# Residual loads and stores of two image pairs at a time in a DMA-bound 3x3 convolution with residual add

## Chip, cores, metric

The kernel runs on one core of a Trainium2 chip. Its time is device time in microseconds (us), the median of several executions. The span is the part of it that the profile covers, from the first to the last instruction recorded. "Outside the span" below is the measured time less the span of the same execution. The runs list every execution's span to 0.1 us; the trace of the profiled execution has it to the nanosecond. The granted clock is the share of its full clock that the tensor engine was allowed, as the trace records it. HBM is the memory off the core, SBUF the core's own (128 partitions in these tiles), and PSUM takes the tensor engine's results here. An execution counts as slow here when it is over 1.5% above the fastest of its kernel.

## The reference

A 3x3 convolution with padding 1 on 16 images of 64 channels and 64x64 pixels, float32, plus a residual of the output's shape.

```python
x_pad = np.pad(x, ((0, 0), (0, 0), (1, 1), (1, 1)))
for b, co, ci, kh, kw in ...:        # 16, 64, 64, 3, 3
    output[b, co] += weight[co, ci, kh, kw] * x_pad[b, ci, kh:kh+h, kw:kw+w]
return output + residual
```

x, residual and output are 16.8 MB each. Every byte crosses between HBM and SBUF once, so 50.3 MB plus 0.15 MB of weights have to move, whatever the order (the profile before has 50.48 MB in its packets).

## The kernel before

The images go through in 8 pairs: 128 partitions hold 2 images of 64 channels, with 4096 pixels (16 KB) in a row. ScalarE casts x to bf16, the tensor engine convolves an image into PSUM, VectorE adds the residual in its own buffer (`ro`), and that buffer is stored. The kernel holds all 8 residual buffers in SBUF at once (16.8 MB). The SP queue issues 25 of the 26 transfers.

```python
ro = [pool.tile([128, NPIX], FP32, name=f"ro{p}") for p in range(NPAIR)]     # 8 pairs
xr = [nc.alloc_sbuf_tensor(f"xr{i}", [128, NPIX], FP32) for i in range(NXR)] # 3 x buffers
...
s_r = [sem(f"s_r{p}") for p in range(NPAIR)]      # one semaphore for each residual
...
for p in range(NPAIR):
    if p >= NXR:
        nc.sync.wait_ge(s_half, 2 * (p - NXR) + 3)   # the x buffer is free again
    ...                                              # x of pair 0 and the weights go first
    load_x(p)                                        # 2 MB
    load_ro(p)                                       # 2 MB
for p in range(NEARLY):                              # 6 early stores
    nc.sync.wait_ge(s_add, 2 * p + 3)
    store(p).then_inc(s_out, 16)
...
for n in range(B):                                   # VectorE, image by image
    if im == 0:
        nc.vector.wait_ge(s_r[p], 16)
    for par in range(2):
        i = nc.vector.tensor_tensor(out=o4[...], in0=psj[...], in1=o4[...], op=ADD)
...
for p in range(NEARLY, NPAIR):                       # the last two pairs
    store(p)
with tc.tile_critical(sync_engine=mybir.EngineType.Pool, no_gpsimd_drain=True):
    nc.gpsimd.wait_ge(s_out, 16 * NEARLY)            # (cuts are marked with ...)
```

Of the kernel before, what the change touches and what calls it, by code (L numbers as in the profile page):

```python
# [8 lines left out]
FP32 = mybir.dt.float32  # L9
# [6 lines left out]
def kernel(  # L16
# [7 lines left out]
    nc = tc.nc  # L24

    B, C, H, W = x.shape
# [4 lines left out]
    NPIX = H * W  # L31
    NPAIR = B // 2
# [2 lines left out]
    NCHUNK = J // JC  # L35
    NXR = 3
    NXP = 4
    NEARLY = 6

    res_bc = residual.rearrange("b c h w -> (b c) (h w)")  # L40
    out_bc = out.rearrange("b c h w -> (b c) (h w)")
    x_bc = x.rearrange("b c h w -> (b c) (h w)")
    w_rows = weight.rearrange("co (h ci) kh kw -> (co h) (ci kh kw)", h=2)

    pool = ctx.enter_context(tc.tile_pool(name="pool", bufs=1))
    psum = ctx.enter_context(tc.tile_pool(name="psum", bufs=1, space=bass.MemoryType.PSUM))

    ident = pool.tile([128, 128], FP32)
    ro = [pool.tile([128, NPIX], FP32, name=f"ro{p}") for p in range(NPAIR)]
    xr = [nc.alloc_sbuf_tensor(f"xr{i}", [128, NPIX], FP32) for i in range(NXR)]  # L50

    xp = [pool.tile([128, J + 1, W], BF16, name=f"xp{i}") for i in range(NXP)]
# [4 lines left out]
    sem = lambda name: tc.alloc_semaphore(name)  # L57
    s_w = sem("s_w")
    s_x = [sem(f"s_x{i}") for i in range(NXR)]
    s_r = [sem(f"s_r{p}") for p in range(NPAIR)]  # L60
    s_out = sem("s_out")
    s_id = sem("s_id")
    s_wt = sem("s_wt")
    s_half = sem("s_half")
    s_pack = sem("s_pack")
    s_bank = sem("s_bank")
# [1 line left out]
    s_add = sem("s_add")  # L68

    def load_x(p, engine=nc.sync, cols=slice(0, NPIX)):  # L70
        return engine.dma_start(out=xr[p % NXR][:, cols], in_=x_bc[128 * p : 128 * p + 128, cols]).then_inc(
            s_x[p % NXR], 16
        )

    def load_ro(p):
        nc.sync.dma_start(out=ro[p][:, :], in_=res_bc[128 * p : 128 * p + 128, :]).then_inc(s_r[p], 16)

    def store(p):
        return nc.sync.dma_start(out=out_bc[128 * p : 128 * p + 128, :], in_=ro[p][:, :])

    def matmul(out_, lhsT, rhs, start, stop, ldweights):

# [18 lines left out]
    def to_the_front(dma):  # L101



        def fixed(ap):
            t = ap.bass_ap.tensor.name
            return mybir.PhysicalAccessPattern(
                ap=ap.ap, offset=ap.bass_ap.offset, dtype=ap.dtype, memref=t, memsetref=t + "_set", bass_ap=ap.bass_ap
            )

        front = nc.main_func.blocks[0].instructions
        here = nc.cur_bb.bb.instructions
        ins = here.pop()
        assert ins.name == dma.ins.name
        at = next(
            i for i, e in enumerate(front) if e.engine == ins.engine and isinstance(e, mybir.InstDrain)
        )
        front.insert(at, copy.replace(ins, ins=[fixed(a) for a in ins.ins], outs=[fixed(a) for a in ins.outs]))
# [5 lines left out]
    def weight_block(h, half, d, par, kh):  # L124

        at = 64 * half + 32 * h
        return dict(out=wl[at : at + 32, d, :, par, :], in_=tp[0:32, kh, 0:384].rearrange("p (kw co h) -> p kw co h", kw=3, h=2)[:, :, :, h])

    with tc.tile_critical(no_gpsimd_drain=True):  # L129

        for p in range(NPAIR):
            if p >= NXR:

                nc.sync.wait_ge(s_half, 2 * (p - NXR) + 3)
            if p == 0:
                to_the_front(load_x(p, cols=slice(0, NPIX // 2)))
                nc.sync.dma_start(out=wraw[:, :], in_=w_rows[:, :]).then_inc(s_w, 16)
            else:
                load_x(p)
            load_ro(p)  # L140
        for p in range(NEARLY):
            nc.sync.wait_ge(s_add, 2 * p + 3)
            store(p).then_inc(s_out, 16)


        nc.gpsimd.memset(ident[:, :], 0.0).then_inc(s_id, 1)  # L146
        nc.gpsimd.wait_ge(s_id, 1)
        nc.gpsimd.affine_select(  # L148
            out=ident[:, :],
            in_=ident[:, :],  # L150
            compare_op=mybir.AluOpType.not_equal,
            fill=1.0,
            base=0,
            pattern=[[-1, 128]],
            channel_multiplier=1,
        ).then_inc(s_id, 1)
        nc.gpsimd.wait_ge(s_id, 2)
        for t in xp:
            nc.gpsimd.memset(t[0:64, 0, :], 0.0).then_inc(s_id, 1)  # L159
            nc.gpsimd.memset(t[64:128, J, :], 0.0).then_inc(s_id, 1)  # L160
        nc.gpsimd.memset(wl[0:64, 0, :, 1, :], 0.0).then_inc(s_id, 1)  # L161
        nc.gpsimd.memset(wl[64:128, 1, :, 0, :], 0.0).then_inc(s_id, 1)  # L162


        to_the_front(load_x(0, nc.scalar, slice(NPIX // 2, NPIX)))
        for n in range(B):
            p, im = divmod(n, 2)
            hp = slice(64 * im, 64 * im + 64)
            x4 = xr[p % NXR].rearrange("q (j two w) -> q j two w", two=2, w=W)
            t = xp[n % NXP]  # L170
            if im == 0:
                nc.scalar.wait_ge(s_x[p % NXR], 16 * (p // NXR + 1 + (p % NXR == 0)))
            i = nc.scalar.copy(out=t[64:128, 0:J, :], in_=x4[hp, :, 0, :])  # L173
            i.then_inc(s_half, 1)
            if n >= NXP:
                i._wait_ge(s_conv, n - NXP + 1)
            nc.scalar.copy(out=t[0:64, 1 : J + 1, :], in_=x4[hp, :, 1, :]).then_inc(s_pack, 1)  # L177
            if n == 0:
                nc.scalar.wait_ge(s_wt, 1)
                for b in blocks[4:]:  # L180
                    for h in range(2):
                        i = nc.scalar.copy(**weight_block(h, *b))  # L182
                i.then_inc(s_wt, 1)


        nc.vector.wait_ge(s_wt, 1)
        for k, b in enumerate(blocks[:4]):
            for h in range(2):
                i = nc.vector.tensor_copy(**weight_block(h, *b))  # L189
                if k == h == 0:  # L190
                    i.then_inc(s_bank, 2)
        i.then_inc(s_wt, 1)
        for n in range(B):
            p, im = divmod(n, 2)
            hp = slice(64 * im, 64 * im + 64)
            o4 = ro[p].rearrange("q (j two w) -> q j two w", two=2, w=W)
            psj = ps[n % 2].rearrange("q c j w -> q (c j) w")
            if im == 0:
                nc.vector.wait_ge(s_r[p], 16)
            for par in range(2):  # L200
                i = nc.vector.tensor_tensor(  # L201
                    out=o4[hp, :, par, :], in0=psj[64 * par : 64 * par + 64, :, :], in1=o4[hp, :, par, :], op=ADD
                )
                if par == 0:
                    i._wait_ge(s_conv, n + 1)

                i.then_inc(s_add if par == 0 or n == B - 1 else s_bank, 1)


        nc.tensor.wait_ge(s_id, 4 + 2 * NXP)  # L210
        nc.tensor.wait_ge(s_w, 16)
        wraw3 = wraw.rearrange("p (ci t) -> p ci t", t=9)
        for t in range(9):
            i = nc.tensor.transpose(  # L214
                out=tp[0:32, t // 3, 128 * (t % 3) : 128 * (t % 3) + 128], in_=wraw3[:, :, t], identity=ident[:, :]
            )
        i.then_inc(s_wt, 1)
        nc.tensor.wait_ge(s_wt, 3)
        with nc.Fori(0, B // NXP, 1, engines=[PE]):
            for n in range(NXP):  # L220
                nc.tensor.wait_ge(s_bank, 1).then_inc(s_bank, -1)
                nc.tensor.wait_ge(s_pack, 1).then_inc(s_pack, -1)  # L222
                order = [(1, 0), (1, 1), (0, 0), (0, 1), (2, 0), (2, 1)]
                for i, (kw, d) in enumerate(order):
                    xlo, xhi = max(0, 1 - kw), min(W, W + 1 - kw)
                    for c in range(NCHUNK):
                        j0 = JC * c
                        m = matmul(
                            ps[n % 2][:, c, :, xlo:xhi],
                            wl[:, d, kw, :, :].rearrange("q r c -> q (r c)"),  # L230
                            xp[n][:, j0 + d : j0 + d + JC, xlo + kw - 1 : xhi + kw - 1],
                            i == 0,
                            i == len(order) - 1,
                            c == 0,
                        )
                m.then_inc(s_conv, 1)


    for p in range(NEARLY, NPAIR):
        store(p)  # L240
    with tc.tile_critical(sync_engine=mybir.EngineType.Pool, no_gpsimd_drain=True):
        nc.gpsimd.wait_ge(s_out, 16 * NEARLY)

# [29 lines left out]
```

## Time and profile before

| | before |
|---|---|
| time, median (first 3 executions) | 122.96 us |
| span of the profiled execution | 121.2 us |
| outside the span (same execution) | 123.0 - 121.2 = 1.8 us |
| bytes moved | 50.48 MB |
| rate, 4 to 76 us and 82 to 119 us | 432 and 431 GB/s |
| tensor engine busy, ends at | 72%, about 100 us |
| VectorE's last add ends at | 104.1 us |
| arrival of the last store: mean of the 16 DMA engines, slowest | 119.87, 120.21 us |

To read it: compute is over at 104 us, and the remaining 16 us are stores that wait in a full queue (the last two are issued at 104.4 and 104.8 us). The time goes by bytes divided by a rate that hardly varies in the two long stretches (432 and 431 GB/s). The last row comes from the trace's records of semaphore increments by the DMA engines: each of the 26 transfers ends in 16 of them (416 small packets in all), taken here as one from each of the 16 engines, and it counts as landed with the slowest.

### The profile page before, as it was taken

The numbers are of one execution on the slowest core, as the hardware profiler recorded it, in microseconds if no ns is written. First come the engines' busy times: TensorE is split into PE (matmuls) and PEld (weight loads), VectorE is DVE, ScalarE is ACT, GpSimd is POOL, SyncE is SP. The second block draws the span as 40 slices with busy tenths as digits, with TensorE's granted clock in tenths as the row PEclk, the third lists the DMA queues.
The fourth block names the chain that finished last, engine by engine and source line by source line (L and its number), as shares of the span: only waits on it lengthen the run. The fifth ranks groups of instructions, "written<-read, shape, count | busy, mean of one in ns | idle before, by whom it ended". The sixth has DMA issues, their size and how long they took to land.

```text
span 121.2 us, 736 instructions
## 1 busy us (share of the span) xinstructions
PE 87.7 (72%) x389; PEld 10.7 (9%) x105; DVE 76.0 (63%) x40; ACT 63.1 (52%) x37; POOL 2.4 (2%) x16
## 2 busy tenths in 40 slices
PE   0033499999999999999999999999999980000000
PEld 0021001101010101010101010101010100000000
DVE  0005300889898898989889898898989889300000
ACT  4049969938966984993993994896000000000000
POOL 5200000000000000000000000000000000000000
PEclk9999999999999999999999999999999999755555
DMA  6999999999999999999999999999999999999993
GB/s 168 427 444 433 433 433 433 433 427 433 433 427 427 433 433 427 427 433 427 433 433 433 433 433 422 433 389 433 433 433 433 422 433 433 433 433 433 427 433 151
DMA packets 3744, 50.48 MB, mean 417 GB/s; under 512 B 416, under 2 KB 544, under 8 KB 544
## 3 DMA queue, kind: packets, MB, share of 16 engines
q1 hardware_dynamic: 3600, 49.43, 96.3%
q10 hardware_dynamic: 144, 1.05, 2.0%
HBM read 33.70 MB, written 16.78 MB: 417 GB/s over the span
## 4 chain that ended last, share of the span: by engine, by line
PE 71%; DVEq 2%; DVE 2%; issue 0%
PE ps L86 53%; PE ps L85 17%; DVEq L129 2%; DVE ro L201 2%
## 5 line engine op out<-in xcount | busy, mean ns | idle before, releaser
L201 DVE TENSOR_TENSOR ro<-ps,ro 64x2048 f32<-64x2048 f32 x32 | 73.2, 2289 | 17.7 <-PE ps L86 17.2
L86 PE MATMUL ps<-xp,wl 128*128 128x504 bf16 (+1 forms) x288 | 80.0, 388 | 0.2
L173 ACT CAST xp<-xr 64x2048 bf16<-64x2048 f32 x16 | 30.3, 1896 | 19.3 <-DMA xr<-in_x_dram 17.1
L85 PE MATMUL ps<-xp,wl 128*128 128x504 bf16 (+1 forms) x92 | 35.8, 389 | 3.4 <-PEq L222 3.4
L177 ACT CAST xp<-xr 64x2048 bf16<-64x2048 f32 x16 | 30.4, 1897 | 0.4
L85 PEld LDWEIGHTS ps<-xp,wl 128*128 128x128 bf16 x96 | 9.5, 99 | 79.1 <-issue 79.1
L189 DVE CAST wl<-ps 32x192 bf16<-32x192 f32 x8 | 2.8, 348 | 10.4 <-PE ps L214 10.3
L214 PE MATMUL ps<-ident,wraw 128*32 128x128 f32 x9 | 2.1, 412 | 8.1 <-DMA wraw<-in_weight_dram 8.1
L214 PEld LDWEIGHTS ps<-ident,wraw 128*32 128x32 f32 x9 | 1.2, 137 | 8.6 <-issue 8.1
L173 ACT ACT_TABLE_LOAD x1 | 1.3, 1283 | 1.1 <-SPq L129 1.1
L182 ACT CAST wl<-ps 32x192 bf16<-32x192 f32 x4 | 1.2, 306 | 0.0
L160 POOL MEMSET xp<- 64x64 bf16 x4 | 0.6, 147 | 0.2
L159 POOL MEMSET xp<- 64x64 bf16 x4 | 0.6, 145 | 0.2
L148 POOL TENSOR_SCALAR_AFFINE_SELECT ident<-ident 128x128 f32<-128x128 f32 x1 | 0.3, 295 | 0.2 <-POOL ident L146 0.2
L162 POOL MEMSET wl<- 64x192 bf16 x1 | 0.3, 253 | 0.1
L161 POOL MEMSET wl<- 64x192 bf16 x1 | 0.3, 252 | 0.1
L146 POOL MEMSET ident<- 128x128 f32 x1 | 0.2, 205 | 0.7 <-SPq L129 0.7
L257 POOL MEMSET const-uint8-127<- 128x1 uint8 x1 | 0.1, 113 | 0.0
L257 POOL MEMSET const-bfloat16-1.0<- 128x1 bf16 x1 | 0.1, 112 | 0.0
L257 POOL MEMSET const-float32-1.0<- 128x1 f32 x1 | 0.1, 109 | 0.0
L257 POOL MEMSET const-float32-0.0<- 128x1 f32 x1 | 0.1, 104 | 0.2 <-issue 0.2
## 6 DMA issues: line engine op xcount, KB each, us to landing
ro<-in_residual_dram SPq DMA_DIRECT2D x8, 2048.0 KB, 21.9
out_dram<-ro SPq DMA_DIRECT2D x8, 2048.0 KB, 28.2
xr<-in_x_dram SPq DMA_DIRECT2D x7, 2048.0 KB, 17.5
xr<-in_x_dram SPq DMA_DIRECT2D x1, 1024.0 KB, 7.0
xr<-in_x_dram ACTq DMA_DIRECT2D x1, 1024.0 KB, 7.6
wraw<-in_weight_dram SPq DMA_DIRECT2D x1, 144.0 KB, 6.9
```

The lines of the kernel that those rows point to most:

```text
L85: return e.matmul(out=out_, lhsT=lhsT, rhs=rhs, start=start, stop=stop, skip_group_check=True)
L86: return e.add_instruction(mybir.InstMatmult(name=nc.get_next_instruction_name(), engine=PE, ins=[e.lower_ap(rhs), e.lower_ap(lhsT)], outs ...
L129: with tc.tile_critical(no_gpsimd_drain=True):
L159: nc.gpsimd.memset(t[0:64, 0, :], 0.0).then_inc(s_id, 1)
L160: nc.gpsimd.memset(t[64:128, J, :], 0.0).then_inc(s_id, 1)
L173: i = nc.scalar.copy(out=t[64:128, 0:J, :], in_=x4[hp, :, 0, :])
L177: nc.scalar.copy(out=t[0:64, 1 : J + 1, :], in_=x4[hp, :, 1, :]).then_inc(s_pack, 1)
L182: i = nc.scalar.copy(**weight_block(h, *b))
L189: i = nc.vector.tensor_copy(**weight_block(h, *b))
L201: i = nc.vector.tensor_tensor(out=o4[hp, :, par, :], in0=psj[64 * par : 64 * par + 64, :, :], in1=o4[hp, :, par, :], op=ADD)
L214: i = nc.tensor.transpose(out=tp[0:32, t // 3, 128 * (t % 3) : 128 * (t % 3) + 128], in_=wraw3[:, :, t], identity=ident[:, :])
L257: nc = _bacc.Bacc("TRN2", target_bir_lowering=False, num_devices=1)
```

## The change

The intent: fewer, larger transfers (residuals of pairs 2-3, 4-5 and 6-7 in one load of 4 MB each; pairs 0-1, 2-3 and 4-5 in one store of 4 MB each), x of the odd pairs loaded one transfer earlier, the last two pairs still stored one by one, and fewer semaphores to clear. Cut to its core:

```diff
-    NEARLY = 6
-    res_bc = residual.rearrange("b c h w -> (b c) (h w)")
+    NEARLY = 3
+    RES = (slice(0, 1), slice(1, 2), slice(2, 4), slice(4, 6), slice(6, 8))
+    res_bc = residual.rearrange("(p b) c h w -> (b c) p (h w)", b=2)
-    ro = [pool.tile([128, NPIX], FP32, name=f"ro{p}") for p in range(NPAIR)]
+    ro = pool.tile([128, NPAIR, NPIX], FP32)
-    s_r = [sem(f"s_r{p}") for p in range(NPAIR)]
+    s_r = [sem(f"s_r{i}") for i in range(2)]
-    s_wt = sem("s_wt")                  # its counts move to s_id
...
+    def load_ro(i):
+        if i >= 2:
+            nc.sync.wait_ge(s_r[i % 2], 16 * (i // 2))
+        nc.sync.dma_start(out=ro[:, RES[i], :], in_=res_bc[:, RES[i], :]).then_inc(s_r[i % 2], 16)
+    def store(pairs):
+        return nc.sync.dma_start(out=out_bc[:, pairs, :], in_=ro[:, pairs, :])
...
-            load_ro(p)
-        for p in range(NEARLY):
-            nc.sync.wait_ge(s_add, 2 * p + 3)
-            store(p).then_inc(s_out, 16)
+            if p in (0, 1, 3, 5, 7):
+                load_ro((p + 1) // 2)
+        for k in range(NEARLY):
+            nc.sync.wait_ge(s_add, 4 * k + 5)
+            store(slice(2 * k, 2 * k + 2)).then_inc(s_out, 16)
...
-    for p in range(NEARLY, NPAIR):
-        store(p)
+    for p in range(2 * NEARLY, NPAIR):
+        store(slice(p, p + 1))
```

More of the change, by code (lines that the diff above doesn't have):

```diff
@@ L37 @@
     NXP = 4
-    NEARLY = 6
-    res_bc = residual.rearrange("b c h w -> (b c) (h w)")
-    out_bc = out.rearrange("b c h w -> (b c) (h w)")
+    NZERO = 4 + 2 * NXP
+    NEARLY = 3
+    RES = (slice(0, 1), slice(1, 2), slice(2, 4), slice(4, 6), slice(6, 8))
+    res_bc = residual.rearrange("(p b) c h w -> (b c) p (h w)", b=2)
+    out_bc = out.rearrange("(p b) c h w -> (b c) p (h w)", b=2)
     x_bc = x.rearrange("b c h w -> (b c) (h w)")
@@ L73, in load_x @@
         )
-    def load_ro(p):
-        nc.sync.dma_start(out=ro[p][:, :], in_=res_bc[128 * p : 128 * p + 128, :]).then_inc(s_r[p], 16)
-    def store(p):
-        return nc.sync.dma_start(out=out_bc[128 * p : 128 * p + 128, :], in_=ro[p][:, :])
+    def load_ro(i):
[4 more added lines that the diff above has]
+        return nc.sync.dma_start(out=out_bc[:, pairs, :], in_=ro[:, pairs, :])
     def matmul(out_, lhsT, rhs, start, stop, ldweights):
@@ L178 @@
             if n == 0:
-                nc.scalar.wait_ge(s_wt, 1)
+                nc.scalar.wait_ge(s_id, NZERO + 1)
                 for b in blocks[4:]:
@@ L182 @@
                         i = nc.scalar.copy(**weight_block(h, *b))
-                i.then_inc(s_wt, 1)
-        nc.vector.wait_ge(s_wt, 1)
+                i.then_inc(s_id, 1)
+        nc.vector.wait_ge(s_id, NZERO + 1)
         for k, b in enumerate(blocks[:4]):
@@ L191 @@
                     i.then_inc(s_bank, 2)
-        i.then_inc(s_wt, 1)
+        i.then_inc(s_id, 1)
+        first = [pairs.start for pairs in RES]
         for n in range(B):
@@ L195 @@
             hp = slice(64 * im, 64 * im + 64)
-            o4 = ro[p].rearrange("q (j two w) -> q j two w", two=2, w=W)
+            o4 = ro[:, p, :].rearrange("q (j two w) -> q j two w", two=2, w=W)
             psj = ps[n % 2].rearrange("q c j w -> q (c j) w")
-            if im == 0:
-                nc.vector.wait_ge(s_r[p], 16)
+            if im == 0 and p in first:
+                i = first.index(p)
+                nc.vector.wait_ge(s_r[i % 2], 16 * (i // 2 + 1))
             for par in range(2):
@@ L207 @@
                 i.then_inc(s_add if par == 0 or n == B - 1 else s_bank, 1)
-        nc.tensor.wait_ge(s_id, 4 + 2 * NXP)
+        nc.tensor.wait_ge(s_id, NZERO)
         nc.tensor.wait_ge(s_w, 16)
@@ L216 @@
             )
-        i.then_inc(s_wt, 1)
-        nc.tensor.wait_ge(s_wt, 3)
+        i.then_inc(s_id, 1)
+        nc.tensor.wait_ge(s_id, NZERO + 3)
         with nc.Fori(0, B // NXP, 1, engines=[PE]):
```

## The prediction

> **What bounds the kernel now.** I read the summary by engine and by slice first. The tensor engine is busy for 72% of the span and nothing else on chip reaches that, but the row to read is the one of the DMA engines:
>
> ```profile
> PE   0033499999999999999999999999999980000000
> ...
> DMA  6999999999999999999999999999999999999993
> GB/s 168 427 444 433 433 433 433 433 427 433 433 427 427 433 433 427 427 433 427 433 433 433 433 433 422 433 389 433 433 433 433 422 433 433 433 433 433 427 433 151
> ```
>
> The tensor engine ends in slice 33 of 40, at about 100 us; the DMA engines run at the same rate from the second slice to the last but one. So the bytes are the clock of this kernel. Next come the DMA queues, and then the busy time by stretch:
>
> ```profile
> DMA packets 3744, 50.48 MB, mean 417 GB/s; under 512 B 416, under 2 KB 544, under 8 KB 544
> ...
> q1 hardware_dynamic: 3600, 49.43, 96.3%
> q10 hardware_dynamic: 144, 1.05, 2.0%
> ```
>
> ```profile
> core 0: us, PE busy (x) PEld busy (x) DVE busy (x) ACT busy (x) POOL busy (x), PEclk, DMA share, GB/s
> 0.00:4.00 4.00, 0.00 (x0) 0.00 (x0) 0.00 (x0) 1.28 (x1) 2.32 (x16) 1.00 0.73 231
> 4.00:76.00 72.00, 64.26 (x283) 8.14 (x79) 50.94 (x30) 54.24 (x32) 0.07 (x1) 1.00 1.01 432
> 76.00:82.00 6.00, 6.00 (x29) 0.68 (x7) 5.39 (x3) 5.69 (x3) 0.00 (x0) 1.00 0.98 396
> 82.00:119.00 37.00, 17.43 (x80) 1.85 (x19) 19.69 (x9) 1.90 (x2) 0.00 (x0) 0.80 1.01 431
> 119.00:121.20 2.20, 0.00 (x0) 0.00 (x0) 0.00 (x0) 0.00 (x0) 0.00 (x0) 0.50 0.09 37
> ```
>
> The last two columns say that the 16 engines are fully busy (share 1.01) at 431 to 432 GB/s from 4 to 76 us and from 82 to 119 us. There are three losses: the first microseconds (231 GB/s), the change from loads to stores between 76 and 82 us (396 GB/s), and about 2 us at the end. The chain that ended last is of little use here. It names tensor lines for 71%, and then at 104 us it meets the vector engine and stops, because the final stores are behind it:
>
> ```profile
> PE ps L86 53%; PE ps L85 17%; DVEq L129 2%; DVE ro L201 2%
> ```
>
> The waits of the queue that issues the DMAs complete the picture: it waits for buffers and results, while its earlier transfers keep the engines fed.
>
> ```profile
> SPq L71 <- ACT xp L173: 51.4, 5, 15.7
> SPq L79 <- DVE ro L201: 24.9, 4, 10.0
> ```
>
> The trace's landing records give each transfer's arrival. Residual pair 2 lands at 32.33 us, x of pair 3 at 37.23, residual pair 3 at 42.08, x of pair 4 at 46.98, residual pair 7 at 81.26, and the eight stores at 86.18, 91.04, 95.91, 100.77, 105.63, 110.50, 115.36 and 120.21. In steady state a 2 MB transfer lands every 4.86 us: 2.097 MB / 4.864 us = 431 GB/s, the rate of the stretch table. There is one exception, the last load (81.26 - 76.18 = 5.08 us).
>
> [...] 8 residual loads, 8 stores, 9 x loads and 1 weight load are 26 transfers, and 26 x 16 = 416 packets, exactly the count under 512 B. [...] with the queue full, 2 MB transfers land 4.86 us apart, which is 8 packets of 16 KB per engine at 608 to 611 ns. [...]
>
> **The change part by part.**
>
> *Fewer, larger transfers.* Residual loads go from 8 to 5 and stores from 8 to 5 (three of 4 MB, two of 2 MB), so 26 transfers become 20. The data is the same, in the same 16 KB rows (each partition's row of one image channel), so 3,200 of 3,200 data packets should stay. What goes is 6 x 16 = 96 semaphore packets. In the trace's packet records one takes 9 ns, so each of the 16 engines saves 6 x 9 = 54 ns. The bubble around it cannot be much more, as 8 x 608 ns = 4.864 us is already the whole landing interval. I count **0.05 us**. The queue's issue instructions (332 to 580 ns each) become fewer and perhaps longer, but they are hidden behind full queues: the final stores, issued at 104.4 and 104.8 us, wait for their predecessors, which land until 110.5.
>
> *x loads further ahead.* The order was x0 r0 x1 r1 x2 r2 x3 r3 x4 r4 ...; it becomes x0 r0 x1 r1 x2 x3 r23 x4 x5 r45 x6 x7 r67. So x of pairs 3, 5 and 7 arrives one transfer (4.86 us) earlier, the even ones at the same time. Residual pairs come only with the second of the two. r23 lands at 42.08 us (as residual 3 did) and the vector engine first needs it for image 4: its adds start every 5.19 us from 21.72 us, so at 42.46 us. It arrives 0.38 us early, the tightest spot of the plan. r45 lands at about 61.5 for image 8 at 63.21, r67 at about 81.2 for image 12 at 83.96. So the tensor engine's pace should not change, and an earlier x only lengthens ScalarE's idle time elsewhere: it waits 17.1 us for x now, and the tensor engine does not wait for it after the start.
>
> *Stores of two pairs.* A store of 4 MB may start when its second pair is added. All loads stand ahead in the queue until 81.2 us. By then the first two are ready (after images 4 and 8, about 45 and 66 us), and they carry 4 x 4.86 = 19.5 us of transfer, to about 100.6. The third needs image 12's first half, which is added at 83.96 + 2.28 = 86.2 us: 14 us early. It reaches to about 110.3; the single last stores are issued near 104.5, so there is 5.8 us of reserve and no hole. Storing the last pairs singly keeps this: both are issued as before.
>
> *13 semaphores instead of 20.* Waiting on a merged semaphore costs the same instruction. The two transfers that wait for an earlier residual (r23 for r0, and so on) wait for things landed long before. At the end Pool clears the range of semaphores in one instruction, on the path to the span's end:
>
> ```profile
> L268 POOLq EVENT_SEMAPHORE_RANGE_CLEAR  x1: 200/200/200, 120.7 to 120.7; - x1
> ```
>
> If its 200 ns scales with the number (the records name semaphores from 96 to 127, some 30), 7 fewer are 7/30 x 200 = 47 ns; if it is fixed, nothing. I count half, **0.03 us**.
>
> *Unchanged:* the start (x0, weights, residual 0 and 1 in the same order), the turn from loads to stores (packet records: the packets that start from 76 to 80 us take 0.38 us per engine more than at 608 ns, once), the 0.34 us from the last packet's end at 119.87 to its landing at 120.21, the closing barriers, and the 1.8 us between the span of 121.2 and the measured 123.0 us.
>
> Sum: 122.96 - 0.05 - 0.03 = 122.88; I lean a little lower for small things at the turn, **122.85 us**.
>
> **The rivals.**
> *A fixed cost per transfer really is in series.* Then six fewer transfers would save six times it[...]. The landing intervals and a DMA share of 1.01 speak against it, as there is no idle time to win.
> *The larger transfers leave a hole.* If r23 came late, or a 4 MB store waited too long, the queue would run dry. A late r23 first delays the vector engine, which has 0.57 us to spare per image, then the tensor engine; only a delay of over 5 us would reach the last stores. A slip of a few tenths is likely, a hole is not; a badly timed one would make perhaps 124 to 126 us.
> *Two rows 2 MB apart in one transfer run slower in HBM.* A partition now has two 16 KB rows 2 MB apart. If packets took 1% longer, 33.5 MB or 78 us of transfer would add up to 0.8 us, 123.7. Against: the engines run at one rate for reads and writes alike (432 and 431 GB/s), so the memory's side does not seem to bind.
> *The turn from loads to stores gets cheaper or dearer.* Its whole loss is 0.4 us, so 122.5 to 123.2.
>
> **Range and chances.** The three runs before lie within 0.18 us. The expected gain of 0.1 us is below what matters, and only the second and third rival move more than the noise. I take 122.5 to 123.2 us, with 1% for faster by over 2% (under 120.5, which needs bytes to vanish or a much better rate) and 1% for slower by over 2% (over 125.4, which needs a hole of 2.4 us).
>
> **What would show it.** In the profile of the changed kernel: under 512 B 320 packets instead of 416; 50.48 MB as before; DMA share 1.01 and 431 to 432 GB/s from 4 to 76 and from 82 to 119 us; the vector engine's adds still 5.19 us apart with image 4 at 42.5 us; last add over at 104.1; the range clear at 200 ns or about 150; span 121.0 to 121.2. I am wrong if the landing interval of 2 MB shrinks below 4.8 us, if the DMA row shows a slice under 9 between 81 and 118 us, or if the vector engine waits for the residual at image 4.

Cuts in it are marked: passages on how the hardware behaves that no trace or run of this case shows, among them a size for the cost per transfer of the first rival. The sum: 122.96 - 0.05 - 0.03 = 122.88, leaned to 122.85 us, with the 0.05 from packets of 9 ns and the 0.03 from the 200 ns of the clear, both of the trace before. That a wait on a merged semaphore costs nothing more, merged_13 below (ratio 1.0007) bears out.

## The result, and the profile after

The changed kernel took 123.17 us in the median of 6 runs (122.97 to 123.42), the kernel before 123.00 us beside it (6 runs, 122.86 to 123.52). The ratio is 1.0008, with a 95% interval of 0.9985 to 1.0031: the same. A ratio is the mean time of one kernel's fast runs over that of the other's of the same rounds, so it is not quite the ratio of the medians. The repetition on another chip with more runs gave 1.0019 (1.0005 to 1.0032). The time lies in the predicted range, but near its upper end, and the small gain that was forecast is not there.

The summary by slice, of the changed kernel (tenths of each slice busy, then GB/s):

```profile
PE   0023499999999997999999999999999960000000
...
DMA  6999999999999999999999999999999999999992
GB/s 184 416 443 427 432 432 427 432 432 432 432 432 432 432 432 432 432 432 432 432 427 432 432 432 432 432 389 432 432 432 432 432 432 432 432 432 427 432 432 108
```

Its DMA queues (packets, bytes, share of the engines' span), and its stretches (the columns are those of the prediction's table; the last two are DMA share and GB/s):

```profile
DMA packets 3648, 50.48 MB, mean 416 GB/s; under 512 B 320, under 2 KB 448, under 8 KB 448
...
q1 hardware_dynamic: 3504, 49.43, 96.1%
q10 hardware_dynamic: 144, 1.05, 2.1%
```

```profile
0.00:4.00 4.00, 0.00 (x0) 0.00 (x0) 0.00 (x0) 1.28 (x1) 2.33 (x16) 1.00 0.75 238
4.00:76.00 72.00, 63.74 (x287) 8.10 (x79) 51.31 (x30) 56.02 (x33) 0.06 (x1) 1.00 1.01 432
76.00:82.00 6.00, 6.00 (x29) 0.68 (x7) 5.39 (x3) 5.58 (x4) 0.00 (x0) 1.00 1.00 410
82.00:119.00 37.00, 17.12 (x80) 1.85 (x19) 19.33 (x9) 0.23 (x1) 0.00 (x0) 0.77 1.01 431
119.00:121.20 2.20, 0.00 (x0) 0.00 (x0) 0.00 (x0) 0.00 (x0) 0.00 (x0) 0.50 0.02 7
```

The picture is the same as before. There are 96 small packets fewer, the rate of the two long stretches is the same to 1 GB/s, and there is no hole anywhere. The turn from loads to stores (76 to 82 us) moves 410 instead of 396 GB/s, and after 119 us there is less left to do (7 instead of 37 GB/s, which over 2.2 us is 0.07 MB less), so the engines are ahead on average. The chain that ended last is again cut at the final stores (and reaches back only to 47 us, 43% on tensor lines instead of 71%); the lines below show it, then the waits of the issuing queue, and the clear of the semaphores:

```profile
PE ps L89 32%; PE ps L88 11%; DVEq L132 2%; DVE ro L207 2%
```

```profile
SPq L72 <- ACT xp L177: 50.6, 5, 16.0
SPq L82 <- DVE ro L207: 27.5, 2, 20.3
```

```profile
L274 POOLq EVENT_SEMAPHORE_RANGE_CLEAR  x1: 158/158/158, 120.8 to 120.8; - x1
```

The clear takes 158 instead of 200 ns. One line is new, in the waits of the engines (total, times, longest):

```profile
DVE ro L207 <- PE ps L89: 15.3, 14, 7.3
...
DVE ro L207 <- DMA ro<-in_residual_dram: 1.4, 1, 1.4
```

VectorE waited 1.4 us for a residual, once, at image 4. That residual (pairs 2 and 3) landed at 42.09 us as predicted (42.08), but in this execution the tensor engine was ahead: the first add began at 20.57 us instead of 21.72. The matmuls of 17 to 20 us (third column: time and number), before and then after, show why:

```profile
17.00:20.00 3.00, 3.00 (x11) 0.24 (x2) 0.00 (x0) 2.19 (x2) 0.00 (x0) 1.00 1.02 437
```

```profile
17.00:20.00 3.00, 3.00 (x16) 0.29 (x3) 0.00 (x0) 2.16 (x2) 0.00 (x0) 1.00 0.99 426
```

In the same 3 us 16 matmuls begin instead of 11: the full rate came earlier. (The column with the granted clock prints 1.00 in both rows because it has no record yet; the trace's first record of a full clock is at 19.10 us before and at 16.73 after.) The earlier clock is not the change: the same program with seven unused semaphores (pad_7 below) has its full clock from 19.40 us and 10 matmuls there, its adds start at 21.85 us, and it does not wait at image 4. The wait needs both, an early clock and the late residual of the change: order_only below, which loads residual 2 alone, starts its adds at 20.75 us and waits for no residual. Over the profiles the first record of a full clock lies between 16.69 and 19.40 us. The wait moved the later adds by 0.8 us (20.57 + 15 x 5.187 = 98.37 us would be the start of the last image, 99.16 was measured), and it cost nothing at the end: the last add still ended at 103.77 us, earlier than before (104.13).

**Where the time went.** Nothing of the above explains why the measured time is 0.17 us more. The listed spans show where it is. On the chip of the repetition:

| | measured, mean | span, mean | outside the span |
|---|---|---|---|
| before (11 runs) | 123.13 | 121.32 | 1.81 (1.78 to 1.87) |
| changed (6 runs) | 123.31 | 121.22 | 2.10 (2.02 to 2.15) |

Within the span the change gains 0.10 us, close to the 0.08 predicted, but with a standard error of 0.08 us (from the listed spans), so by itself this gain is not clear of noise. Outside the span it loses 0.29 us, in every execution, and no range overlaps. The listed spans are rounded; with the exact spans of the fourteen profiled executions (experiments included) the time outside is 1.79 to 1.83 us in the six that load one residual pair at a time and 2.06 to 2.07 in the eight that load two or three, a loss of about 0.24. So the loss is 0.24 to 0.29 us. The experiments look for what does that, and test the bound itself.

### The profile page after: what moved, and what is told of

It reads as the page before. It is cut to its first block, busy times and chain, and to the rows that moved or that the text cites. A ratio compares the mean times of both kernels' runs of the same rounds, so it can differ in the third digit from the quotient of the medians.

```text
span 121.3 us, 731 instructions
## 1 busy us (share of the span) xinstructions
PE 86.9 (72%) x393; PEld 10.6 (9%) x105; DVE 76.0 (63%) x40; ACT 63.1 (52%) x37; POOL 2.4 (2%) x16
```

## The experiments

The theory: bytes at a fixed rate set the span; the number of transfers and their order hardly matter. Its main rival: a fixed cost for each transfer, in series. When the loss outside the span appeared, two further theories stood against each other: the semaphores do it, or the transfers of two pairs do.

### split_halves: 64-partition transfers (an experiment that tested something else)

```diff
-        nc.sync.dma_start(out=ro[p][:, :], in_=res_bc[128 * p : 128 * p + 128, :]).then_inc(s_r[p], 16)
+        for h in (0, 64):
+            nc.sync.dma_start(
+                out=ro[p][h : h + 64, :], in_=res_bc[128 * p + h : 128 * p + h + 64, :]
+            ).then_inc(s_r[p], 16)
```

(from the kernel before; not shown: stores likewise, counts of the waits doubled)

> Edit of the kernel before: every residual load and every store is cut into two transfers of 64 partitions (1 MB each), so 42 transfers instead of 26, with the same 16 KB rows. Theory (the bytes set the time, a transfer costs each engine only its 9 ns semaphore packet): 16 x 9 = 0.14 us more, 123.1 us, 672 small packets instead of 416, a DMA share still at 1.01. Rival (a cost per transfer that stands in series): 16 times that cost; at 0.5 us it would be 131 us[...].

Measured: 171.58 us in the median, ratio 1.378 (1.370 to 1.386) from fast runs. Two of its six runs are fast (168.46 and 170.82), the profiled one is slow (172.11). At first sight this is the rival's victory, but the stretches of its profile say otherwise:

```profile
8.00:12.00 4.00, 2.08 (x9) 1.16 (x9) 0.92 (x3) 3.82 (x3) 0.00 (x0) 1.00 1.01 213
12.00:16.00 4.00, 1.64 (x4) 0.26 (x2) 1.86 (x6) 3.92 (x6) 0.00 (x0) 1.00 1.08 225
...
156.00:160.00 4.00, 0.00 (x0) 0.00 (x0) 0.00 (x0) 0.00 (x0) 0.00 (x0) 0.50 1.02 434
```

While residual halves are loaded (first two rows) the engines are busy all the time (share 1.01 and 1.08; a packet's time is counted where it starts, so a share can pass 1) at half the rate, 213 to 225 GB/s. A cost in series for each transfer should, by the author's reasoning, have left the engines idle. The packet records agree: while residual halves move, a 16 KB packet takes some 1250 ns instead of 611. Why a load of 64 partitions goes at half the rate is not shown. The stores in halves (last row) ran at 422 to 438 GB/s from 148 us on, with packets of 611 ns, while the 16 engines were up to 5.9 us apart (one landing runs from 156.15 to 162.05 us); so the halving is shown for the loads, and why late stores escape it is not shown either. So the split changed more than the count, and the question went to col_split.

### col_split: the same count, all 128 partitions

```diff
-        nc.sync.dma_start(out=ro[p][:, :], in_=res_bc[128 * p : 128 * p + 128, :]).then_inc(s_r[p], 16)
+        for c in (slice(0, NPIX // 2), slice(NPIX // 2, NPIX)):
+            nc.sync.dma_start(out=ro[p][:, c], in_=res_bc[128 * p : 128 * p + 128, c]).then_inc(s_r[p], 16)
```

(from the kernel before; not shown: stores likewise, counts of the waits doubled)

> Edit of the kernel before: every residual load and store is cut in two by columns, over all 128 partitions (1 MB, rows of 8 KB), so again 42 transfers instead of 26. It repeats split_halves without its fault: there 64-partition transfers took 1250 ns for a 16 KB packet in place of 611. Theory (a transfer costs 9 ns per engine): 0.14 us for 16 more transfers, and 256 packets of 8 KB per engine at 309 ns in place of 128 of 16 KB at 611 ns, 0.9 us: 123.2 + 1.0 = 124.2 us at most. Rival (0.5 us or more per transfer in series): 131 us or more.

Measured: 123.44 us, ratio 1.0023 (1.0004 to 1.0041), span 121.60 instead of 121.34 us on average. Its packets:

```profile
DMA packets 6048, 50.48 MB, mean 415 GB/s; under 512 B 672, under 2 KB 800, under 8 KB 800
```

Sixteen transfers more, and twice as many data packets of half the size, cost 0.26 us together, 16 ns a transfer if all of it is laid on the count. The rival of a serial cost of half a microsecond or more is out. This is why six transfers fewer can bring so little.

### order_only: the new order of loads alone

```diff
-            load_ro(p)
+            if p < 2:
+                load_ro(p)
+            elif p % 2:
+                load_ro(p - 1)
+                load_ro(p)
```

> Edit of the kernel before: the order of loads of the changed kernel (x further ahead, residuals two by two) but as single 2 MB transfers with their own semaphores; stores as before. Theory: 123.0 us, the time does not depend on the order. Residual 2 lands at about 37.2 us instead of 42.1 in the changed kernel, so the vector engine does not wait for a residual at image 4, unlike in the changed kernel (1.4 us there). Rival (the order of loads cost what the fewer packets saved): 123.1 us or more, with the spread of the engines of the changed kernel.

Measured: 123.16 us, ratio 1.0007 (0.9991 to 1.0023), outside the span 1.80 us. Residual 2 landed at 37.33 us and VectorE waited for no residual. "x loads further ahead" is worth nothing measurable here (the rival's "123.1 us or more" is no sign of it: the kernel before took 123.18 beside it). The loss outside the span does not come from the order.

### after_again: the changed kernel once more

> The changed kernel once more, unedited, for a tighter ratio and a second profile. Theory: 0.999 to 1.001. In the first profiles the 16 engines finished their last data packet at 119.52 us on average before and 119.34 after, but the slowest one at 119.87 before and 120.00 after. If that spread comes from how a single execution starts, this profile has another spread (first to last arrival of the x of pair 0 between 0.5 and 0.9 us) and the average stays at 119.3 to 119.4. If the change makes the spread, it is again 0.8 us after the start and 0.98 us for the stores.

Measured: 123.33 us, ratio 1.0019 (1.0005 to 1.0032). Its ratio is a little above the expected bound of 1.001. The 16 engines finished the first x within 0.60 us of each other this time (0.73 in the first profile), and the last store within 0.78 us (0.98); the mean over the engines of the last data packet's end was 119.25 us, the slowest 119.81. So the spread of the first profile belonged at least in part to that execution.

### res_three: how much delay the compute side can take

```diff
-    RES = (slice(0, 1), slice(1, 2), slice(2, 4), slice(4, 6), slice(6, 8))
+    RES = (slice(0, 1), slice(1, 2), slice(2, 5), slice(5, 6), slice(6, 8))
```

> Edit of the changed kernel: residual pairs 2, 3 and 4 in one transfer of 6 MB. Theory (compute has about 5.8 us of reserve before the last two stores would find the queue empty): the transfer lands at about 46.95 us, the vector engine waits for it some 5 us at image 4, the last add ends at about 108.7 us instead of 103.8, store of pair 6 is issued at about 109.0 and its data can start about 1 us later, just when the queue empties (110.0): 122.9 to 123.4 us. Rival (a wait of the vector engine for a residual goes straight to the end): 5 us more, 128 us.

Measured: 125.50 us, ratio 1.017 (1.0138 to 1.0201), so more than the theory's 123.4 and less than the rival's 128. The load landed at 46.96 us as expected, but the last add ended at 111.02 us, not at 108.7. The stretches (third column tensor engine, then from the right GB/s, DMA share, granted clock):

```profile
48.00:52.00 4.00, 0.00 (x0) 0.07 (x1) 3.94 (x3) 0.08 (x1) 0.00 (x0) 0.75 0.99 422
52.00:56.00 4.00, 3.67 (x9) 0.33 (x3) 3.97 (x2) 3.95 (x3) 0.00 (x0) 0.50 1.04 446
...
108.00:112.00 4.00, 0.00 (x0) 0.00 (x0) 2.99 (x2) 0.00 (x0) 0.00 (x0) 0.93 0.33 139
```

The tensor engine was idle for 4.6 us, and restarted at half its clock (0.50): 9 matmuls began in 4 us. The clock records have it at half from 50.00 to 56.82 us. The half clock cost about 2.9 us on top of the wait: the adds of images 5 and 6 are 8.04 us apart, not 5.19. The store of pair 6 was issued at 111.31 us, and between 108 and 112 us the queue ran dry (share 0.33). The span of this execution is 123.41 us; that of after_again, on the same chip, is 121.22 on average, 2.19 us less. So the store could have been issued until about 111.31 - 2.19 = 109.12 us without loss. Against pad_7 below, an undelayed kernel whose adds start at the same time (21.85 us) and which issues this store at 104.56, that is an estimated reserve of 4.6 us; the prediction had 5.8 us, and left out that data follow an issue by about 1 us (the first packet of the span starts 1.01 us after the first issue, that of this store 0.85 us after its issue). The mechanism holds in these two kernels: the late residual cost nothing at the end in the changed one (a wait of 1.4 us, last add at 103.77 us), while here, together with the half clock after it, it cost 2.19 us of the span, as the final stores found the queue empty.

### pad_7, merged_13, sems_40: do the semaphores make the loss outside the span?

pad_7, from the changed kernel (back to 20 semaphores):

```diff
+    unused = [sem(f"unused{i}") for i in range(7)]
```

> What is to be explained: in eleven timed executions of the kernel before on one chip the measured time less the span is 1.78 to 1.87 us, in six of the changed kernel 2.02 to 2.15 us, so the changed kernel gains some 0.2 us within the span and gives back 0.3 us outside it; the kernel with only the new order of loads has 1.78 to 1.84. Edit of the changed kernel: 7 unused semaphores are added, so 20 again. Theory A (the number or numbering of semaphores sets the time outside the span): back to 1.8 us outside, range clear back to 200 ns, total 122.85 to 122.95 us. Theory B (the 4 MB transfers or the program's layout set it): stays at 2.1 us, total 123.3 us.

merged_13, from the kernel before (down to 13):

```diff
-    s_r = [sem(f"s_r{p}") for p in range(NPAIR)]
+    s_r = [sem(f"s_r{i}") for i in range(2)]
-    s_wt = sem("s_wt")                  # its counts move to s_id, as in the change
...
+        if p >= 2:
+            nc.sync.wait_ge(s_r[p % 2], 16 * (p // 2))
...
```

(not shown: the counts that the other engines wait for)

> Edit of the kernel before: its 20 semaphores are merged into 13 exactly as in the changed kernel (two for the residuals, the one of the weights joined to the one of the zeros), transfers and their order unchanged. Theory A (semaphores set the time outside the span): 2.1 us outside, range clear 158 ns, total 123.35 us. Theory B (4 MB transfers or layout): 1.8 us outside, total 123.1 us.

sems_40, from the changed kernel, the line of pad_7 with 40:

> Edit of the changed kernel: 40 unused semaphores are added. If the range clear goes by number, at (200 - 158) / 7 = 6 ns each, it takes 158 + 240 = 398 ns, all of it in the span; if it is a step or fixed it stays near 158 to 200 ns. Time outside the span: with theory A it differs from 2.1 us, with theory B it is 2.1 us.

Measured: pad_7 123.38 us, outside the span 2.10; merged_13 123.27 us (ratio 1.0007, 0.9984 to 1.0029, so its merged waits cost nothing measurable), outside 1.83; sems_40 123.58 us, outside 2.08. Theory A falls three times: the time outside the span does not follow the number of semaphores. Theory B is left, with the transfers and the layout not yet told apart. What the semaphores do cost is the clear, here of sems_40:

```profile
L275 POOLq EVENT_SEMAPHORE_RANGE_CLEAR  x1: 374/374/374, 121.0 to 121.0; - x1
```

It took 157 ns in merged_13, 158 with 13 in the changed kernel, 200 in pad_7, and 374 with 53: 5 to 6 ns for each semaphore ((374 - 158) / 40 = 5.4), at the very end of the span. Seven fewer save 0.04 us.

### loads_single and stores_single: which transfers make it?

loads_single, from the changed kernel (residuals one pair a load again, 4 MB stores kept):

```diff
+    RES = tuple(slice(p, p + 1) for p in range(8))
...
-            if p in (0, 1, 3, 5, 7):
-                load_ro((p + 1) // 2)
+            if p < 2:
+                load_ro(p)
+            elif p % 2:
+                load_ro(p - 1)
+                load_ro(p)
```

> So far every kernel with 4 MB transfers has 2.08 to 2.10 us of measured time outside the span on average (four of them, with 13, 20 and 53 semaphores) and every kernel with 2 MB or smaller ones 1.80 to 1.84 (20 or 13 semaphores). Edit of the changed kernel: residuals again one pair a transfer, in the same order; stores stay at 4 MB. If the loads of 4 MB cost the time outside: 1.8 us, total 122.95 to 123.05 us, below the kernel before. If the stores cost it, or the residuals' single large tile: 2.1 us, total 123.3 us. If each shares: about 1.95.

stores_single, from the changed kernel (stores one pair each, 4 MB loads kept):

```diff
-    NEARLY = 3
+    NEARLY = 6
...
-            nc.sync.wait_ge(s_add, 4 * k + 5)
-            store(slice(2 * k, 2 * k + 2)).then_inc(s_out, 16)
+            nc.sync.wait_ge(s_add, 2 * k + 3)
+            store(slice(k, k + 1)).then_inc(s_out, 16)
...
```

(not shown: the last two stores count from NEARLY again)

> Edit of the changed kernel: all stores again one pair a transfer; residual loads stay at 4 MB. If the stores of 4 MB cost the time outside: 1.8 us, total 122.95 to 123.1 us. If the loads or the single tile cost it: 2.1 us, total 123.3 to 123.4 us. The turn from loads to stores is also read here: with 2 MB stores behind it, it cost 0.28 to 0.41 us per engine in three profiles, with 4 MB loads and stores 0.17 to 0.24 in five; if the stores' size does that, here it is 0.3 to 0.4.

Measured, on the same chip: loads_single 123.03 us (122.92 to 123.17), ratio 0.9991 (0.9976 to 1.0005), outside 1.82; stores_single 123.25 us (123.11 to 123.53), ratio 1.0011 (0.9995 to 1.0026), outside 2.12. The loss comes from the residual loads of two pairs alone; neither the stores of two pairs nor the one large tile have it. loads_single has no loss outside the span, and within it its mean of 121.22 us is 0.11 below the kernel before beside it (standard error 0.06). It is 0.2 us faster than stores_single beside it; against the kernel before its interval includes 1, so it is not shown to beat that. On the turn, my expectation for stores_single fell: 0.17 us per engine, not 0.3 to 0.4.

### cols_of_two: size or pattern?

```diff
-        nc.sync.dma_start(out=ro[:, RES[i], :], in_=res_bc[:, RES[i], :]).then_inc(s_r[i % 2], 16)
+        for c in (slice(0, NPIX // 2), slice(NPIX // 2, NPIX)) if i >= 2 else (slice(0, NPIX),):
+            nc.sync.dma_start(out=ro[:, RES[i], c], in_=res_bc[:, RES[i], c]).then_inc(s_r[i % 2], 16)
```

(from the changed kernel; not shown: the counts of the waits follow)

> The residual loads of 4 MB bring 0.28 us outside the span (2.12 us with them and single stores, 1.82 us with single loads and 4 MB stores). Edit of the changed kernel: each 4 MB residual load becomes two of 2 MB that still take two pairs each, half of the columns (rows of 8 KB), so the pattern with two pairs stays and the size goes back. If the size of 4 MB costs the time outside: 1.82 us, total 123.1 us. If the pattern over two pairs (or its 256 rows a transfer) costs it: 2.1 us, total 123.4 us. Within the span: three more semaphore packets per engine (27 ns) and 96 rows of 8 KB per engine instead of 48 of 16 KB; the cut by columns of all loads and stores cost 0.27 us within the span, so about 0.1 us here.

Measured: 122.98 us beside 123.00, ratio 1.0001 (0.9987 to 1.0014); outside the span 2.10 us, span 120.90 beside 121.19. Loads of 2 MB over two pairs have the loss as well, so 4 MB is not its cause: it is the pattern over two pairs, or the 256 rows that such a load has where a load of one pair has 128. These two were not told apart. The number of transfers is out as well: loads_single, stores_single and cols_of_two have 23 each (368 small packets) and 13 semaphores, and only the first is free of the loss. Rows of 8 KB are not the cause either, as col_split has them without it (1.84 us). Why such loads cost time that the profile does not cover stays open. It does not show as longer closing steps: the trace's semaphore records go on for 1.94 us after the span's end both before and in cols_of_two.

The expected longer span did not come: it is the shortest of all, 0.29 us below the kernel before (standard error 0.05). The packets of the turn from loads to stores were stretched by only 0.02 us per engine (counted as in the section on the prediction below, for packets of 8 KB above 309 ns), and so they were in col_split, the other kernel whose residual loads have 8 KB rows. The ten kernels whose residuals come in 16 KB rows over all 128 partitions have 0.10 to 0.41.

### last_pair: the last two pairs in one store

```diff
-    for p in range(2 * NEARLY, NPAIR):
-        store(slice(p, p + 1))
+    store(slice(2 * NEARLY, NPAIR))
```

> Edit of the changed kernel: the last two pairs are stored in one transfer of 4 MB too, as the others. Theory (they are issued at 104.4 and 104.8 us, long before the queue empties at about 110): the same span within 0.1 us, 121.1 to 121.3, so storing them singly brings nothing. Rival (the last single stores shorten the end): 0.3 us or more longer.

Measured: 123.59 us, ratio 1.0039 to the kernel before (1.0021 to 1.0057), span 121.53 us on average beside 121.15 and 121.22 of stores_single and loads_single. The rival was right. The waits of the SP queue, of the changed kernel and then of last_pair (total, times, longest):

```profile
SPq L274 <- DMA out_dram<-ro: 15.1, 2, 10.3
```

```profile
SPq L273 <- POOLq L246: 15.9, 1, 15.9
```

In the changed kernel SP is released by the last store itself: GpSimd, which ends the program, had seen the store of pair 6 land at 115.50 us and gone through its own closing steps by 116.04, while pair 7 was still being written. With one store it can only begin at 120.08, and SP waits for GpSimd. From the last landing to the end of the span it is 121.39 - 120.08 = 1.31 us, instead of 121.26 - 120.35 = 0.91. Storing the last pairs singly is worth 0.3 us. The kernel before did so too, so it is a part that the change was right to keep and no part of its gain.

## Why the prediction was right or wrong

**Right: bytes set the time.** The range of 122.5 to 123.2 us held, with 123.17 us. That it held is partly luck, by 0.03 us: the repetition took 123.33 us, above the range, on a chip where the kernel before took 123.18. The long stretches run at 432 and 431 GB/s before and after, there is no hole, the small packets are 320 as counted, and col_split bounds the cost of a transfer at 16 ns, near the 9 ns of the estimate. The rival of a serial cost per transfer was rightly dismissed.

**Right in size, as far as the noise lets one see: the gain within the span.** The sum said 0.08 us; the spans of the repetition differ by 0.10 us, with a standard error of 0.08. The spans of pad_7, loads_single and stores_single are 0.07, 0.11 and 0.18 us below the kernel before beside them, the same sign each time. The terms of the sum were less exact. The clear of semaphores saved 42 ns, not the 30 counted (the 47 ns of the scaling were nearer). The semaphore packets saved their 54 ns per engine.

**Missed within the span, with both signs.** "Unchanged ... the turn from loads to stores": it changed. Counting for 16 KB packets that start from 70 to 84 us what they take above 611 ns, per engine: 0.36 us before, 0.28 in order_only and 0.41 in merged_13; but 0.24 and 0.17 in the two profiles of the changed kernel, 0.17 in loads_single and in stores_single. So about 0.15 us were gained there; neither two-pair loads nor two-pair stores alone do it, since loads_single and stores_single have it too, and what does is not shown. In the first profile it is eaten again by the spread of the engines. In that pair of profiles the mean arrival of the last store is 119.87 before and 119.67 after, that of the slowest engine 120.21 and 120.35; only the slowest counts. It is partly an accident of each execution (merged_13, with single transfers, has 119.87 and 120.62). Whether two-pair transfers widen the spread, these single profiles do not settle. At the landing of the first load and of the last store the 16 engines are apart by 0.61 and 0.55 us before, 0.73 and 0.98 after, and 0.51 and 1.08 in merged_13, where it grew to 1.0 us at the turn from loads to stores; the smallest at the last store, 0.24 us, is in res_three, whose queue had just run dry.

**Wrong: "Unchanged ... the 1.8 us between the span of 121.2 and the measured 123.0 us."** This step failed. The 1.8 us became 2.10 (2.06 with exact spans). These 0.24 to 0.29 us are larger than the whole gain and turned 0.1 us of gain into 0.18 us of loss (123.31 - 123.13); they are also most of the 0.32 us between the forecast of 122.85 and the measured 123.17. The runs put it down to the residual loads over two pairs:

| kernel | residual loads | stores | semaphores | outside the span, mean (runs) |
|---|---|---|---|---|
| before | one pair | one pair | 20 | 1.81 (11) |
| order_only | one pair | one pair | 20 | 1.80 (4) |
| merged_13 | one pair | one pair | 13 | 1.83 (6) |
| loads_single | one pair | two pairs | 13 | 1.82 (6) |
| after_again | two pairs | two pairs | 13 | 2.10 (6) |
| pad_7 | two pairs | two pairs | 20 | 2.10 (6) |
| sems_40 | two pairs | two pairs | 53 | 2.08 (4) |
| stores_single | two pairs | one pair | 13 | 2.12 (6) |
| cols_of_two | two pairs, half the columns | two pairs | 13 | 2.10 (5) |

The other runs fit: split_halves and col_split, one pair a load, 1.81 and 1.84 us; res_three and last_pair, with loads of two or three pairs, 2.10 and 2.07. That the loads do it is shown; the mechanism stays open.

**Wrong by the prediction's own sign: image 4.** "I am wrong ... if the vector engine waits for the residual at image 4." It did, for 1.4 us, and again in after_again, cols_of_two and last_pair (0.9, 1.0 and 1.5 us). The forecast of the landing was right within 0.01 us; wrong was the need: it took the first add at 21.72 us as given, while in the four profiles with the wait the first add began at 20.57 to 21.01 us, as the clock rose earlier. So "arrives 0.38 us early" was a statement about one execution. The prediction had also called a slip of a few tenths likely, and rightly held that it would not reach the last stores.

**Off in size: the reserve.** 5.8 us estimated, about 4.6 us by res_three, the microsecond from issue to data left out. (Its sum is also 0.1 us low: 81.2 + 19.5 is 100.7, not 100.6.) Nor had I counted, in res_three's expectation, that the tensor engine would come back from its 4.6 us of idling at half clock (0.50, from 50.00 to 56.82 us): there the add of image 4 was late by 47.05 - (37.39 + 5.19) = 4.5 us, and the last add ended at 111.02 us instead of 104.26 in pad_7, 6.8 us later.

**Right by luck: "Storing the last pairs singly keeps this."** The reason given (no hole) is not what single stores bring; last_pair shows that they hide 0.3 us of closing work.

## What to carry to other kernels

With the DMA engines busy at one rate from start to end (share 1.01, 431 to 432 GB/s) and transfers of 2 MB, larger ones and another order of them had next to nothing to win here (ratio 1.0008 for the change, 1.0007 for the order alone): count the small packets they save (96 here, 54 ns per engine), and expect hundredths of a microsecond. At such sizes compare the span and the measured time separately, since a change can gain in one and lose in the other (here 0.10 us gained within the span and 0.29 lost outside). Let the last transfer be a small one of its own, so that closing work runs beside it (0.3 us here), and do not split loads by partition halves (213 to 225 GB/s while such loads ran, 1.38 times the time with stores split too). A margin of a few tenths of a microsecond in one profile was no margin here: the moment at which the clock rose differed by 2.7 us between these profiles (16.69 to 19.40 us).
